# Four more stages as seven quarter products of 256 columns, and the mix loads on GpSimd's queue

## The chip, the cores and the metric

The kernel runs on one core of a Trainium2 chip. The metric is the device time of one execution in microseconds (us). A run's time is compared with the median of the runs of the kernel before, and one execution of each kernel is recorded by the hardware profiler: which instruction ran on which engine, when, and what ended the idle time ahead of it. The engines are TensorE (PE, with its weight loads PEld), VectorE (DVE), ScalarE (ACT), GpSimd (POOL) and SyncE (SP); the last two mostly issue transfers here.

## The reference

One transformer block on 512 tokens of width 1024 in fp32. A vector c gives six modulations (adaLN). The normalised and modulated input is multiplied by w_in; the columns are split into q, k, v of 16 stick-breaking heads (width 64), q, k of 4 retention heads (width 256), v and gate of those heads (width 512) and two branch gates.

```python
mod = jnp.einsum('bd,de->be', c_act, w_ada[l]) + b_ada[l]
hmix = modulate(rmsnorm(x, g_norm1[l]), shift1, scale1)
proj = jnp.einsum('bsd,de->bse', hmix, w_in[l])
sb_q, sb_k, sb_v, r_q, r_k, r_v, r_g, br = jnp.split(proj, IN_SPLITS, axis=-1)
...
# per retention head: scores with a decay mask, outputs, rms norm, times silu(gate)
# per stick-breaking head: log_sigmoid of the scores, a running sum, exp, times v
```

Both attentions are projected (w_proj_sb, w_proj_ret), weighted by the sigmoids of the branch gates, added, projected by w_out and added to x; then comes a gated feed-forward network (FFN) with its own modulation, and a final normalisation.

## The kernel before, in words

Every matrix is kept as a pair of rounded values, a high half and a low half (high = the value rounded to the fast fp32r format, low = the rest). A product is three matmuls: high x high, high x low, low x high (`mm3`, all recorded at line L229). A weight piece of 128 x 1024 elements (512 KB) is loaded by SP's queue into a buffer `raw` (three buffers) or `araw` (two), ScalarE makes its high half `whi` and VectorE subtracts to get the low half `wlo` (four buffers each; `split`, L207 and L209). The activations of the input stage are eight pairs `hs` with the features on the partitions.

Some products are already done by Strassen and Winograd's scheme: seven products of quarter size with sums of weights and of activations in place of eight. The sums of the activations, with their high and low halves, lie ready in `sacts` under the names A11, A12, A22, S1 to S4. `seven("r2", ...)` makes the values of heads 1 and 2 that way, `seven("sv", ...)` the stick-breaking values, both with 512 columns per matmul, and the FFN with 256. `low_dma` (L869, L870) is a second way to a low half: ScalarE writes the negated high half and an accumulating transfer from GpSimd's queue adds the raw weight to it.

The stages around the change, with their times in the profiled execution: the gate of head 1 (194 to 218 us), q and k of head 2, the projection of head 1 (about 240 to 262), outputs of head 2, the gate of head 2 (273 to 297), q and k of head 3, values of head 3 (319 to 341, `ret_v`), the projection of head 2, outputs of head 3, the gate of head 3 (376 to 399), the projection of head 3 (399 to 421), the stick-breaking values (`seven("sv")`, 421 to 459), then `sb_qk(0)`, a mix, `sb_qk(1)`, a mix (459 to 492), the stick-breaking heads with the remaining mixes, the loop over w_proj_sb (730 to 775), the loop over w_out and the FFN (830 to 1125). A mix reads a sum of projections back from memory (`spill`), multiplies it by a branch gate and writes it again.

`ret_gate` makes four products of 128 columns of the gate with 24 matmuls of 512 tokens each; between the second and the fourth stand a column sum and a broadcast (`ret_scale`, `bcast`) that normalise the retention output. Each silu'd gate multiplies an output tile on VectorE, which is then split into high and low halves (`s`) for the projection. Partial results of the projections are added in memory by transfers on GpSimd's queue (L816).

The adaLN modulations that are not needed at once (16 calculations) are spread over later stages by `ada_after`: two loads of 512 KB into `araw` and two dot products on VectorE (L257, 128 x 1024) each, with small additions (L260). The loop over w_proj_sb loads two tiles `r` and `t` per step, L1123 and L1124.

The program is written in a framework whose scheduler fixes the order of each engine's instructions when the program is built; at run time each engine takes them in that order and waits at the first that is not ready.

## Time and profile before

| what | value |
|---|---|
| median of 3 runs | 1174.38 us (1173.70 to 1174.75) |
| profiled execution, its own time | 1174.77 us |
| its span (first to last instruction) | 1173.1 us |
| mean granted TensorE clock | 0.998 of full speed |
| matmuls recorded | 6476 |
| ScalarE busy | 52% |

The page lists busy time by engine, the chain of work that ended last, groups of equal instructions and the transfers. A row of a group reads: line, engine, operation, output<-input, partitions x elements, xcount, then busy time in all, mean of one in ns, and the engine's idle time just ahead with what ended it. A row of the timeline reads: start, length, engine, line, operation, with the idle time ahead in brackets. A matmul's row in the timeline includes its way through the array, so its price in a row of equal ones is taken from the distance of starts. A stretch lists busy time of PE, PEld, DVE, ACT and POOL in a window.

### The profile page before, as it was taken

To read this page: it belongs to the slowest core of one execution; us is meant where nothing else is said; L and a number is where in the kernel's file an instruction comes from. 1 tells how busy PE (TensorE), PEld (TensorE's weight loads), DVE (VectorE), ACT (ScalarE), POOL (GpSimd) and SP (SyncE) were. 2 spreads that over 40 slices of the span, in tenths; PEclk is the share of its full clock that TensorE was granted. 3 is DMA by queue.
4 is the path that set the end of the run, shared out by engine and by line. 5 is a ranking of instruction groups with operands and counts; after the bars stand their busy time and mean duration, and the time that the engine had idled before them with its cause. 6 is when DMAs were issued, how large, how long until landed. Compare 5 with 4: busy or idle time off the path is not lost.

```text
span 1173.1 us, 16899 instructions
## 1 busy us (share of the span) xinstructions
PE 1156.8 (99%) x6476; PEld 1010.9 (86%) x6476; DVE 873.2 (74%) x1342; ACT 611.9 (52%) x928; POOL 50.1 (4%) x84
## 2 busy tenths in 40 slices
PE   8999999999999999999999999999999999999996
PEld 7898888888878888888888888879999999999996
DVE  7979966775764867478888688775998776777556
ACT  5444543343333444478778688354954444454433
POOL 0000000020002010000000000000100000000000
PEclk9999999999999999999999999999999999999999
DMA  9723536493566565846565545873545663565232
GB/s 358 256 68 113 185 103 208 154 260 115 161 201 176 181 159 185 232 123 180 153 173 133 153 126 179 283 235 103 113 136 179 184 161 116 148 186 152 86 89 72
DMA packets 64017, 192.88 MB, mean 164 GB/s; under 512 B 7744, under 2 KB 9920, under 8 KB 63936
## 3 DMA queue, kind: packets, MB, share of 16 engines
q1 hardware_dynamic: 56624, 172.92, 46.3%
q0 software_dynamic: 6768, 18.35, 8.8%
q8 instruction: 51, 0.84, 0.3%
q10 hardware_dynamic: 544, 0.52, 0.1%
q14 instruction: 30, 0.25, 0.1%
HBM read 146.15 MB, written 18.87 MB: 141 GB/s over the span
## 4 chain that ended last, share of the span: by engine, by line
PE 89%; DVE 4%; DMA 3%; ACT 2%; issue 1%; SPq 0%; DVEq 0%; ACTq 0%
PE ps L229 65%; PE z L229 21%; PE av L229 3%; DMA raw<-wp 2%; DMA araw<-wada 1%; DVE sraw L387 1%; ACT whi L207 1%; DVE wlo L209 1%; DMA o<-xT 0%; ACT s L207 0%; DVE wlo L418 0%; DVE t L425 0%; DVE araw L257 0%; DMA gspill<-g 0%; DVE t L476 0%
## 5 line engine op out<-in xcount | busy, mean ns | idle before, releaser
L229 PE MATMUL ps<-h,whi 128*128 128x512 f32 (+1 forms) x1410 | 416.9, 377 | 1.6 <-DVE h L209 0.8
L229 PEld LDWEIGHTS ps<-h,whi 128*128 128x128 f32 x1410 | 256.2, 188 | 47.7 <-ACT h L431 1.8
L229 PE MATMUL ps<-h,wlo 128*128 128x512 f32 (+1 forms) x705 | 262.1, 376 | 0.0
L207 ACT ACTIVATE whi<-raw 128x1024 fp32r<-128x1024 f32 (+1 forms) x122 | 127.4, 1044 | 192.3 <-PE ps L229 144.8
L209 DVE TENSOR_TENSOR wlo<-raw,whi 128x1024 fp32r<-128x1024 f32 (+1 forms) x122 | 146.6, 1204 | 61.9 <-ACT whi L207 60.8
L229 PEld LDWEIGHTS ps<-h,wlo 128*128 128x128 f32 x705 | 132.8, 188 | 23.2
L229 PE MATMUL ps<-s,whi 128*128 128x512 f32 x480 | 148.5, 390 | 0.7 <-DVE v L209 0.6
L229 PE MATMUL z<-q,whi 128*128 128x256 f32 x504 | 106.8, 283 | 0.0
L229 PEld LDWEIGHTS ps<-s,whi 128*128 128x128 f32 x480 | 89.2, 188 | 19.3 <-DVE v L209 1.0
L229 PE MATMUL ps<-s,wlo 128*128 128x512 f32 x240 | 93.4, 389 | 0.0
L207 ACT ACTIVATE s<-t 128x512 fp32r<-128x512 f32 (+1 forms) x134 | 74.4, 586 | 34.8 <-DVE t L789 21.4
L209 DVE TENSOR_TENSOR s<-t,s 128x512 fp32r<-128x512 f32 (+1 forms) x134 | 81.3, 637 | 9.6 <-ACT s L207 9.3
L229 PEld LDWEIGHTS z<-q,whi 128*128 128x128 f32 x504 | 84.9, 192 | 1.5
L1166 DVE SCALAR_TENSOR_TENSOR o<-ps,mod,o 128x512 f32<-128x512 f32 (+1 forms) x63 | 42.4, 680 | 32.6 <-PE ps L229 32.6
L229 PEld LDWEIGHTS ps<-s,wlo 128*128 128x128 f32 x240 | 45.1, 188 | 9.5
L877 ACT ACTIVATE whi<-s 128x1024 fp32r<-128x1024 f32 x33 | 34.9, 1056 | 33.6 <-PE ps L229 19.0
L229 PE MATMUL ps<-whi,h 128*128 128x512 f32 (+1 forms) x192 | 52.4, 354 | 0.0
L881 DVE TENSOR_TENSOR wlo<-s,whi 128x1024 fp32r<-128x1024 f32 x32 | 39.1, 1222 | 16.3 <-ACT whi L877 15.9
L229 PE MATMUL ps<-q,whi 128*128 128x256 f32 (+1 forms) x224 | 49.3, 313 | 0.0
L229 PE MATMUL z<-qp,whi 128*128 128x256 f32 x168 | 47.2, 283 | 0.0
L229 PE MATMUL z<-q,wlo 128*128 128x256 f32 x168 | 46.4, 283 | 0.0
L257 DVE SCALAR_TENSOR_TENSOR araw<-araw,cact 128x1024 f32<-128x1024 f32 x32 | 38.4, 1221 | 10.0 <-DMA araw<-wada 9.8
(311 smaller groups left out, 2063.1 us busy)
## 6 DMA issues: line engine op xcount, KB each, us to landing
raw<-wp SPq DMA_DIRECT2D x151, 512.0 KB, 4.0
araw<-wada SPq DMA_DIRECT2D x32, 512.0 KB, 4.5
araw<-wp SPq DMA_DIRECT2D x26, 512.0 KB, 4.6
sraw<-wada SPq DMA_DIRECT2D x16, 512.0 KB, 7.8
q<-qp SPq DMA_DIRECT2D x32, 256.0 KB, 3.7
s<-wp SPq DMA_DIRECT2D x12, 512.0 KB, 5.2
spill<-o POOLq DMA_DIRECT2D x24, 256.0 KB, 7.2
o<-xT SPq DMA_DIRECT2D x16, 256.0 KB, 3.7
```

The lines of the kernel that those rows point to most:

```text
L207: nc.scalar.activation(dst_hi, src, AF.Copy, scale=scale)
L209: return (eng or nc.vector).tensor_sub(dst_lo, src, f(dst_hi))
L229: return nc.tensor.matmul(o, lhs, rhs, start=start, stop=stop, skip_group_check=True).ins
L257: nc.vector.scalar_tensor_tensor(raw, raw, 1.0, cact, op0=ALU.mult, op1=ALU.mult, accum_out=col)
L387: nc.vector.scalar_tensor_tensor(raw, raw, 1.0, cact, op0=ALU.mult, op1=ALU.mult, accum_out=col)
L877: nc.scalar.activation(hi, t, AF.Copy)
L881: nc.vector.tensor_sub(lo, t, f(hi))
L1166: return nc.vector.scalar_tensor_tensor(x1[d][:, hv], o[:, hv], mod[:, gcol + d : gcol + d + 1], x1[d][:, hv], op0=ALU.mult, op1=ALU.add,)
```

## The change

Four stages are now made by a new function `unit`: the gates of heads 1 and 2 (`rg1`, `rg2`), the values of head 3 (`rv3`) and q and k of the stick-breaking pairs 0 and 1 together (`sb0`). A unit has 512 rows of the weight, twice, by 512 columns, twice: four raw pieces b11, b12, b21, b22 of 512 KB (512 x 256 elements each), from which seven weight operands are made (w1 to w7), and seven products of 24 matmuls with 256 columns each. Three of the operands are raw pieces, four are sums on VectorE. w3's low half is made by the negated copy and the accumulating transfer. The seven results are summed into the four quarter outputs by VectorE (with two copies by ScalarE), and each is handed to `store` as it is done. For the values the activations are the stationary operand (`tokens=True`), otherwise the weights.

`unit_gate` normalises the output tiles between the products, multiplies each by silu of its quarter outputs and splits a tile when both its halves are there. `unit_sb` splits q and k of both pairs into four tiles and spreads them over the heads by transfers when the unit is done; both mixes follow it, where one stood after each pair before. The loads and the first three operands of `sb0` are written into `seven("sv")`, ahead of its last product.

The adaLN calculations are taken from the gates of heads 1 and 2 and added to the gate of head 3 (after each of its four tiles, not after every second) and, since the same list is worked off, to the loop over w_proj_sb: the gates have 2, 2, 2 before and 0, 0, 4 now, the loop 2 before and 4 now, the projections of heads 1 and 2 four each as before. The loads of `r` and `t` in that loop go from SP's queue to GpSimd's.

```diff
--- before.py
+++ after.py
@@ -41,6 +41,15 @@
 FF_CHUNKS = ((0, 1), (1, 2), (3, 2), (5, 2), (7, 2), (9, 2))
 
 
+
+UNITS = {
+    "rg1": (C_RG + 1 * RV, C_RG + 1 * RV + 256),
+    "rg2": (C_RG + 2 * RV, C_RG + 2 * RV + 256),
+    "rv3": (C_RV + 3 * RV, C_RV + 3 * RV + 256),
+    "sb0": (C_Q, C_K),
+}
+
+
 def weight_plan():
 
     plan = []
@@ -58,6 +67,10 @@
             for c in range(2):
                 for piece in range(2):
                     add((name, half, c, piece), "w_in", half * 512 + piece * 256, 2, rng(col + c * 512, 512))
+    for name, cols in UNITS.items():
+        for half in range(2):
+            for c in range(2):
+                add(("u", name, half, c), "w_in", half * 512, 4, rng(cols[c], 256))
     for p in range(8):
         add(("sq", p), "w_in", 0, 8, rng(C_Q + p * P, P))
         add(("sk", p), "w_in", 0, 8, rng(C_K + p * P, P))
@@ -560,6 +573,9 @@
         qhl, khl = pair("qp"), pair("qp")
         split(qhl[:, 0, :], qhl[:, 1, :], qp, 0.125)
         split(khl[:, 0, :], khl[:, 1, :], kp)
+        sb_qk_spread(p, qhl, khl)
+
+    def sb_qk_spread(p, qhl, khl):
         kt_ = pair("q")
         for hf in range(2):
             r = slice(hf * HD, hf * HD + HD)
@@ -791,7 +807,7 @@
             ins = split(hl[:, 0, :], hl[:, 1, :], t)
             ys.append(hl)
             between()
-            if e % 2 and h:
+            if h == 3 or h == 1 and e % 2:
                 ada_after(ins)
         return ys
 
@@ -978,6 +994,122 @@
                 split(t4[:, :, 0:4:3, :], t4[:, :, 1:3, :], src)
             if hc:
                 nc.sync.dma_start(vspill[2 * g + n], f(vt))
+
+    def unit_raw(name, half, c, tag):
+        r = wpool.tile([P, WCOLS], F32, tag=tag, bufs=BUFS[tag], name=nm(tag))
+        nc.sync.dma_start(r, wp[WIDX["u", name, half, c]])
+        return r
+
+    def unit_ahead(name):
+
+        b11, b12, b22 = unit_raw(name, 0, 0, "raw"), unit_raw(name, 0, 1, "araw"), unit_raw(name, 1, 1, "raw")
+        w1 = sv_parts(b11)
+        nc.vector.tensor_sub(b11, b12, b11)
+        w5 = sv_parts(b11)
+        b21 = unit_raw(name, 1, 0, "araw")
+        return b11, b12, b22, b21, w1, w5, sv_parts(b21)
+
+    def unit(name, store, hooks={}, tokens=False, ahead=None):
+
+
+
+        def product(key, w, o=None):
+            ah, al = sacts[key]
+            first = o is None
+            o = ps() if first else o
+            hi, lo = (t.rearrange("p (k c) -> p k c", k=4) for t in w)
+            for i in range(2):
+                oi = o[:, i * 256 : i * 256 + 256]
+                c = slice(i * P, i * P + P)
+                for k in range(4):
+                    a, z = first and i == 0 and k == 0, i == 1 and k == 3
+                    if tokens:
+                        mm(oi, ah[k][:, c], hi[:, k, :], a, False)
+                        mm(oi, ah[k][:, c], lo[:, k, :], False, False)
+                        mm(oi, al[k][:, c], hi[:, k, :], False, z)
+                    else:
+                        mm3(oi, hi[:, k, c], lo[:, k, c], ah[k], al[k], a, z)
+            return o
+
+        hook = lambda n: hooks.get(n, lambda: None)()
+        b11, b12, b22, b21, w1, w5, w2 = ahead or unit_ahead(name)
+        x = product("A11", w1)
+        p1, p5, c22 = otile(), otile(), otile()
+        nc.scalar.activation(p1, x, AF.Copy)
+        nc.vector.tensor_sub(b11, b22, b11)
+        w6 = sv_parts(b11)
+        nc.scalar.activation(p5, product("S1", w5), AF.Copy)
+        hook(5)
+        nc.vector.tensor_sub(b12, b22, b12)
+        w7 = sv_parts(b12)
+        nc.vector.tensor_sub(b21, b21, b11)
+        x = product("A12", w2, x)
+        if 6 not in hooks:
+            store(0, 0, x)
+        w3 = sv_parts(b22, True)
+        nc.vector.tensor_add(p1, p1, product("S2", w6))
+        if 6 in hooks:
+            hook(6)
+            store(0, 0, x)
+        nc.vector.tensor_add(p5, p5, p1)
+        w4 = sv_parts(b21)
+        o = product("S3", w7)
+        nc.vector.tensor_add(c22, p5, o)
+        nc.vector.tensor_add(p1, p1, o)
+        store(1, 1, c22)
+        nc.vector.tensor_add(p1, p1, product("A22", w4))
+        store(1, 0, p1)
+        nc.vector.tensor_add(p5, p5, product("S4", w3))
+        store(0, 1, p5)
+
+    def unit_v(h):
+        vt = [pair("v") for _ in range(4)]
+
+        def store(th, c, t):
+            for b in range(2):
+                hl = vt[2 * th + b]
+                cc = slice(c * 256, c * 256 + 256)
+                split(hl[:, 0, cc], hl[:, 1, cc], t[:, b * 256 : b * 256 + 256])
+
+        unit(f"rv{h}", store, tokens=True)
+        return vt
+
+    def unit_gate(h, os_, sq):
+        y, ys, left = [], {}, {0: 2, 1: 2}
+
+        def scale():
+            r = bcast(y[0], psa())
+            for t in os_:
+                nc.vector.tensor_mul(t, t, r)
+
+        def store(th, c, t):
+            sg = tmp()
+            nc.scalar.activation(sg, t, AF.Silu)
+            for i in range(2):
+                o = os_[2 * c + i][:, th * 256 : th * 256 + 256]
+                nc.vector.tensor_mul(o, o, sg[:, i * 256 : i * 256 + 256])
+            left[c] -= 1
+            if left[c] == 0:
+                for e in (2 * c, 2 * c + 1):
+                    ys[e] = pair("s")
+                    last_low[0] = split(ys[e][:, 0, :], ys[e][:, 1, :], os_[e])
+
+        unit(f"rg{h}", store, {5: lambda: y.append(ret_scale(h, sq)), 6: scale})
+        return [ys[e] for e in range(4)]
+
+    def unit_sb(ahead=None):
+
+        hls = [[pair("s"), pair("s")] for _ in PI]
+
+        def store(th, c, t):
+            tt = slice(th * 256, th * 256 + 256)
+            for p in PI:
+                hl = hls[p][c]
+                split(hl[:, 0, tt], hl[:, 1, tt], t[:, p * 256 : p * 256 + 256], 0.125 if c == 0 else 1.0)
+
+        unit("sb0", store, ahead=ahead)
+        for p in PI:
+            sb_qk_spread(p, *hls[p])
 
     rvts = {}
 
@@ -1056,7 +1188,10 @@
         if h == 0:
             steps = sv_acts()
             sacts = next(steps)
-        ys = ret_gate(h, os_, sq, (lambda: next(steps)) if h == 0 else lambda: None)
+        if f"rg{h}" in UNITS:
+            ys = unit_gate(h, os_, sq)
+        else:
+            ys = ret_gate(h, os_, sq, (lambda: next(steps)) if h == 0 else lambda: None)
         if h < 3:
             qk = ret_qk(h + 1)
             scores = lambda: st.update(ret_scores(h + 1, qk))
@@ -1070,10 +1205,11 @@
                 nc.sync.dma_start(f(vt[b]), vspill[4 + b])
             ret_proj(1, ys, lambda i: scores() if i == 3 else None)
         elif h == 2:
-            vt = ret_v(3)
+            vt = unit_v(3) if "rv3" in UNITS else ret_v(3)
             ret_proj(2, ys, lambda i: scores() if i == 3 else None)
     act_table = ln_exp_tables()
-    seven("sv", 3, ys, sv_store)
+    sb0 = []
+    seven("sv", 3, ys, sv_store, lambda: sb0.append(unit_ahead("sb0")) if "sb0" in UNITS else None)
 
     maskc = table(consts[:, NCON + 2 * S :])
 
@@ -1091,8 +1227,11 @@
             fn, d = mixes.pop(0)
             fn(d)
 
+    if "sb0" in UNITS:
+        unit_sb(sb0[0])
     for p in PI:
-        sb_qk(p)
+        if "sb0" not in UNITS:
+            sb_qk(p)
         with tc.issue_after(act_table.ins):
             mix(1)
     for g, n in enumerate((2, 2, 4, 6)):
@@ -1120,8 +1259,8 @@
         o = ps()
         gemm(o, weight(("ps", d)), acts)
         r, t = tmp(), tmp()
-        nc.sync.dma_start(r, spill[d])
-        nc.sync.dma_start(t, gspill[d])
+        nc.gpsimd.dma_start(r, spill[d])
+        nc.gpsimd.dma_start(t, gspill[d])
         nc.vector.tensor_mul(t, t, o)
         nc.vector.tensor_add(t, t, r)
         hl = pair("h")
```

The built order of three places. First ScalarE in the gate of head 1: `whi` are high halves of weights, `t<-ps` at L777 (L1087 after) is silu, `s` the high half of a gated tile. Before:

```order
L207 ACTIVATE whi_380_1991<-raw_379_1989 128x1024
L777 ACTIVATE t_350_1860<-ps_346_1829 128x512
L207 ACTIVATE whi_391_2040<-raw_390_2038 128x1024
L777 ACTIVATE t_360_1915<-ps_356_1884 128x512
L207 ACTIVATE s_366_1932<-t_335_1771 128x512
L207 ACTIVATE s_367_1937<-t_338_1788 128x512
L207 ACTIVATE whi_394_2070<-raw_393_2068 128x1024
```

After, from the same place; L1038 and L1041 copy the first two products out of PSUM, L885 is the negated copy for w3's low half (`wlo_371`):

```order
L893 ACTIVATE whi_360_1880<-raw_346_1829 128x1024
L1038 ACTIVATE o_357_1875<-ps_356_1850 128x512
L893 ACTIVATE whi_368_1933<-araw_347_1831 128x1024
L1041 ACTIVATE o_358_1876<-ps_362_1884 128x512
L893 ACTIVATE whi_370_1962<-raw_348_1833 128x1024
L1087 ACTIVATE t_378_2010<-ps_356_1850 128x512
L885 ACTIVATE wlo_371_1963<-whi_370_1962 128x1024
L893 ACTIVATE whi_379_2015<-araw_353_1844 128x1024
```

The negated copy stands behind the silu of the first quarter output, though its own input, the high half `whi_370`, is written one place ahead of that. On TensorE the scheduler has put three quarters of S4's matmuls, which use that low half, ahead of A22's here, right behind S3's.

Second VectorE in the gate of head 3 (not a unit): `s` at L209 (L222) are the low halves of the gated tiles, `araw` at L257 (L270) the adaLN dots, `wlo` low halves of weights. Before:

```order
L209 TENSOR_TENSOR s_662_3436<-t_631_3275,s_662_3436 128x512
L209 TENSOR_TENSOR s_663_3441<-t_634_3292,s_663_3441 128x512
L257 SCALAR_TENSOR_TENSOR araw_664_3444,sm_665_3446<-araw_664_3444,cact_71 128x1024
L257 SCALAR_TENSOR_TENSOR araw_666_3449,sm_667_3451<-araw_666_3449,cact_71 128x1024
L260 TENSOR_TENSOR mod_95<-sm_665_3446,sm_70 128x1
L789 TENSOR_TENSOR t_637_3310<-t_637_3310,t_672_3485 128x512
L260 TENSOR_TENSOR mod_95<-sm_667_3451,sm_70 128x1
L788 TENSOR_TENSOR t_640_3328<-t_640_3328,av_657_3421 128x512
L209 TENSOR_TENSOR wlo_701_3598<-raw_699_3595,whi_700_3597 128x1024
L209 TENSOR_TENSOR s_673_3489<-t_637_3310,s_673_3489 128x512
```

After, from the first `s` on, with the rows between cut at the second pair of dots:

```order
L222 TENSOR_TENSOR wlo_726_3900<-raw_724_3897,whi_725_3899 128x1024
L270 SCALAR_TENSOR_TENSOR araw_682_3730,sm_683_3732<-araw_682_3730,cact_71 128x1024
L270 SCALAR_TENSOR_TENSOR araw_684_3735,sm_685_3737<-araw_684_3735,cact_71 128x1024
L273 TENSOR_TENSOR mod_95<-sm_683_3732,sm_70 128x1
L222 TENSOR_TENSOR s_692_3777<-t_650_3584,s_692_3777 128x512
L273 TENSOR_TENSOR mod_95<-sm_685_3737,sm_70 128x1
L805 TENSOR_TENSOR t_653_3602<-t_653_3602,t_702_3823 128x512
L280 SCALAR_TENSOR_TENSOR sm_686_3740<-mod_95,sm_70 128x1
L222 TENSOR_TENSOR wlo_735_3942<-raw_733_3939,whi_734_3941 128x1024
L222 TENSOR_TENSOR s_703_3827<-t_653_3602,s_703_3827 128x512
```

A second pair of dots (`araw_682`, `araw_684`) now stands ahead of the low halves of the third tile (`s_692`) and the fourth (`s_703`); before, one pair stood ahead of the third and the other behind the fourth.

Third the loads near the end of the loop over w_proj_sb. SP's queue before, where `raw<-wp` are weights and L1123 and L1124 the mix loads:

```order
L1123 DMA t_1309_6908<-spill_563 128x512
L202 DMA araw_1287_6787<-wada 128x1024
L202 DMA araw_1289_6792<-wada 128x1024
L1124 DMA t_1310_6909<-gspill_564 128x512
L202 DMA raw_1313_6918<-wp 128x1024
L1123 DMA t_1316_6948<-spill_563 128x512
L202 DMA raw_1320_6958<-wp 128x1024
```

SP's queue after, with the weights and the adaLN loads alone:

```order
L215 DMA raw_1364_7390<-wp 128x1024
L215 DMA araw_1323_7199<-wada 128x1024
L215 DMA araw_1325_7204<-wada 128x1024
L215 DMA raw_1371_7430<-wp 128x1024
L215 DMA araw_1334_7249<-wada 128x1024
L215 DMA araw_1336_7254<-wada 128x1024
L215 DMA raw_1390_7494<-wp 128x1024
```

A mix load ahead of a weight has gone from SP's queue, and two adaLN loads stand in its place; the mix loads are the only rows of GpSimd's queue between the low half for `sb0` and the first of the FFN.

## The prediction

> **What bounds the kernel now.** I read the page's head first (span, busy time by engine, shares of the chain that ended last).
>
> ```profile
> span 1173.1 us, 16899 instructions
> PE 1156.8 (99%) x6476; PEld 1010.9 (86%) x6476; DVE 873.2 (74%) x1342; ACT 611.9 (52%) x928; POOL 50.1 (4%) x84
> PE 89%; DVE 4%; DMA 3%; ACT 2%; issue 1%; SPq 0%; DVEq 0%; ACTq 0%
> ```
>
> TensorE is busy 99% of the span and carries 89% of the chain. The table of what TensorE waited for, all program, says how much waiting there is to add to or to win:
>
> ```profile
> PE z L229 <- DVE mod L450: 3.8, 1, 3.8
> PE ps L229 <- DVE h L209: 0.8, 1, 0.8
> ...
> PE ps L229 <- ACT h L431: 0.2, 1, 0.2
> ```
>
> It has 7 rows; after the first, at the start of the program, none is over 0.8 us. So TensorE's time is the program's time nearly everywhere, and a matmul saved is time saved unless a wait takes its place. The stages in question come next, as stretches: length, then busy time of PE, PEld, DVE, ACT and POOL (instructions), the granted clock, the DMA share, GB/s. In order: gate of head 1, gate of head 2, values of head 3, gate of head 3, the q and k products of the first two stick-breaking pairs with their two mixes, the loop over w_proj_sb, and the FFN.
>
> ```profile
> 194.32:218.10 23.78, 23.78 (x113) 19.84 (x112) 16.95 (x39) 7.17 (x11) 0.00 (x0) 1.00 0.57 187
> 273.40:297.20 23.80, 23.80 (x114) 19.83 (x113) 16.69 (x40) 7.16 (x11) 0.00 (x0) 1.00 0.27 86
> 318.90:340.70 21.80, 21.80 (x97) 17.76 (x95) 14.15 (x21) 7.12 (x9) 0.00 (x0) 1.00 0.45 142
> 376.00:399.30 23.30, 23.30 (x111) 19.45 (x110) 15.69 (x38) 7.48 (x11) 0.00 (x0) 1.00 0.31 91
> 458.85:491.50 32.65, 32.65 (x145) 27.04 (x144) 13.90 (x19) 11.38 (x17) 0.00 (x0) 1.00 0.89 245
> 728.00:777.00 49.00, 47.81 (x211) 39.04 (x209) 34.51 (x50) 17.59 (x22) 0.00 (x0) 1.00 0.81 271
> 830.00:1125.00 295.00, 295.00 (x2095) 278.67 (x2094) 221.29 (x250) 147.12 (x175) 16.33 (x19) 1.00 0.54 149
> ```
>
> The first five have no idle TensorE, so each is a stretch where saved matmuls count in full; VectorE is the next fullest (16.95 of 23.78 us in gate 1). The FFN is the precedent: it is already made of seven quarter products with 256 columns, and TensorE never waits in 295 us while VectorE is 75% busy.
>
> **The products.** The price of a matmul comes from runs of equal ones in the chain of waits (start, length, what):
>
> ```profile
> 53.85 7.49 PE ps L229 x62
> 207.44 48.99 PE ps L229 x216
> 850.58 5.76 PE z L229 x48
> ```
>
> 48.99 / 216 = 226.8 ns for 512 columns; 5.76 / 48 = 120.0 ns for 256 columns with the weight as the stationary side; 7.49 / 62 = 120.8 ns for 256 columns with activations stationary, as the values of head 3 have it. The old product is 96 matmuls, 96 x 0.2268 = 21.77 us. A unit is 7 x 24 = 168, so 168 x 0.1200 = 20.16 us (gain 1.61) or 168 x 0.1208 = 20.29 us (gain 1.48, values). Four units: 3 x 1.61 + 1.48 = 6.31 us less TensorE work. It lies on the path.
>
> A rule speaks against that. The Trainium skill, "TensorE: Matmul & The Clock Gate", section "Back-to-back issue gap", gives 81 ns per matmul at 128 columns and 131 ns at 512 for a sustained stream of weight load and matmul, so cost grows far less than in proportion to columns; an estimate on the line between them is 98 ns at 256, by which 168 matmuls of 256 would cost 16.5 us against 12.6 us for 96 of 512, and the change would lose. This trace does not agree: 226.8 and 120.0 ns, a ratio of 0.53, which is near the isolated gap of the same section.
>
> **What the units add off TensorE.** The rows are groups of instructions (xcount | busy, mean ns | idle before):
>
> ```profile
> L209 DVE TENSOR_TENSOR wlo<-raw,whi 128x1024 fp32r<-128x1024 f32 x118 | 143.9, 1222 | 61.6 <-ACT whi L207 60.5
> L207 ACT ACTIVATE whi<-raw 128x1024 fp32r<-128x1024 f32 x118 | 124.9, 1058 | 188.8 <-PE ps L229 143.3 <-issue 21.2 <-DMA raw<-wp 13.8
> L257 DVE SCALAR_TENSOR_TENSOR araw<-araw,cact 128x1024 f32<-128x1024 f32 x32 | 38.4, 1221 | 10.0 <-DMA araw<-wada 9.8
> L788 DVE TENSOR_TENSOR t<-t,av 128x512 f32<-128x512 f32 x16 | 10.6, 680 | 0.0
> ```
>
> VectorE: 4 low halves become 6 low halves and 4 weight sums, 6 more of 1.22 us = 7.3; 6 adds of 128x512 at 0.68 = 4.1; together 11.4 us per unit. ScalarE: 4 high halves become 7 and a negated copy, 4 more of 1.06 = 4.2, and two copies out of PSUM of about half that: 5.3 us per unit. The weights' bytes stay as they are (4 x 512 KB). ScalarE was busy 7 to 11 us in each of those stretches and takes this beside the matmuls. VectorE is tighter. Gates 1 and 2 lose two adaLN calculations each (2 dots of 1.22 us apiece, 4.9 us a gate), so gate 1 comes to 16.95 + 11.4 - 4.9 = 23.5 us of summed durations in 23.78 - 1.61 = 22.2 us. Neighbours on VectorE overlap by some 7% (two weight halves in a row take 2.35 us in a row below, so the second costs 1.13), so it is just full; what is left over runs on into the q/k product behind it, whose weights are split early. I cost the arithmetic itself at nothing, hidden beside the matmuls, in gates 1 and 2 and in the values of head 3 (there 14.15 + 11.4 against 20.3 us; the surplus of 5 us must be done in the q/k stage ahead, where the first weights of the unit can be prepared; if not, it costs up to those 5 us, which belongs to the rivals), and price below the places where one late result meets a matmul.
>
> **Low half of b22 by transfer, gates 1 and 2.** S4 uses a low half made by a negated copy on ScalarE and an accumulating transfer from GpSimd's queue. In a gate S4 is begun after five products and the two small ones of the normalisation, 5 x 2.88 + (23.78 - 21.77) = 16.4 us in, its low half a third of a us later. The negated copy stands behind the silu of A12's result. A12 ends at 3 x 2.88 + some 0.7 = 9.4; silu of 128x512 half of 1.06, then the copy: 11.0. The transfers of that kind, L870, wherever they run (from issue to landing):
>
> ```profile
> DMA to landing us min/median/max: 4.5/5.2/8.5
> ```
>
> It lands at 15.5, 16.2 or 19.5 against 16.7: a stall of 0 at the median and 2.8 at the maximum. I take 0.5 in each of the two gates, nearer the median; ends 0 and 5.6 for both. It can't be below 0, as TensorE waits for nothing there now; that holds for every term but the last. In the values of head 3 and the pairs no silu stands ahead of the copy and S4 comes last: nothing.
>
> **The adaLN dots, moved.** There are now none in gates 1 and 2, four in gate 3 instead of two, four in the loop over w_proj_sb instead of two. Each needs two loads of 512 KB into a pair of buffers (araw) that the units use too, and each dot that waits for its load holds VectorE with all that stands behind it:
>
> ```profile
> 256.74 1.23 DVE L257 SCALAR_TENSOR_TENSOR araw<-araw,cact 128x1024 f32<-128x1024 f32 x1 [5.46 <-DMA araw<-wada]
> 352.55 1.23 DVE L257 SCALAR_TENSOR_TENSOR araw<-araw,cact 128x1024 f32<-128x1024 f32 x1 [3.16 <-DMA araw<-wada]
> 261.80 2.35 DVE L210 SCALAR_TENSOR_TENSOR s<-z,con,s 128x256 fp32r<-128x256 f32 x4
> 265.58 1.63 PE L229 MATMUL z<-s,v 128*128 128x256 f32 x10
> araw<-wada SPq DMA_DIRECT2D x32, 512.0 KB, 4.5
> ```
>
> Before gate 2 a weight sum of the unit now stands between the last dots of the projection of head 1 and the low halves of the scores, which end at 261.80 + 2.35 = 264.15 now. TensorE comes to them at 265.58, with unit 1 at 263.97. If the loads come no sooner, that is 0.2 late, with the sum ahead 1.3; if they move along, nothing: 0 to 1.3, I take 0.3, since a load that lands sooner frees all of it. Gate 3 is the place I trust least:
>
> ```profile
> 392.07 1.28 DVE L209 TENSOR_TENSOR s<-t,s 128x512 fp32r<-128x512 f32 x2
> 393.28 1.22 DVE L257 SCALAR_TENSOR_TENSOR araw<-araw,cact 128x1024 f32<-128x1024 f32 x1
> ...
> 396.91 1.22 DVE L209 TENSOR_TENSOR wlo<-raw,whi 128x1024 fp32r<-128x1024 f32 x1
> 398.04 0.69 DVE L209 TENSOR_TENSOR s<-t,s 128x512 fp32r<-128x512 f32 x1
> ...
> 402.51 0.69 DVE L209 TENSOR_TENSOR s<-t,s 128x512 fp32r<-128x512 f32 x1 [0.70 <-ACT s L207]
> 394.53 1.47 SPq L202 DMA_DIRECT2D araw<-wada  x2
> ```
>
> The second pair of dots will stand ahead of the low halves of the third and fourth gated tile, and its buffers come free only with the first pair of dots. Its loads, issued as in the last row, land 4.5 us later or more: 399 to 402. Then 2.3 us of dots, a 1.1 us weight half and the fourth tile's half follow, so that one is ready at 402.9 to 406.8 instead of at 403.2. The projection of head 3 needs it at about 403.5. Stall 0 to 3; I take 1.2, below the middle, since 4.5 is the median of such loads.
>
> **Stick-breaking pairs.** Both pairs' unit now runs ahead of both mixes, and its preparation inside the last products of the seven-product stage in front. Around the seam VectorE has:
>
> ```profile
> 456.66 2.35 DVE L209 TENSOR_TENSOR wlo<-raw,whi 128x1024 fp32r<-128x1024 f32 x2
> 458.93 1.28 DVE L1048 TENSOR_TENSOR t<-t,ps 128x512 f32<-128x512 f32 x2
> ...
> 461.59 1.43 DVE L209 TENSOR_TENSOR s<-t,s 128x256 fp32r<-128x256 f32 x4
> 474.05 0.60 SPq L568 DMA_DIRECT2D q<-qp  x1
> ```
>
> The unit's third prepared weight (for S2) stands behind the old stage's stores and three sums. By those durations its low half is ready near 468.4; TensorE comes to it at 468.0. I take 0.5 (0 to 1.5). The spread of q and k over the heads is 16 transfers from SP's queue behind the unit, 0.6 us an issue (last row of the fence). In the old times the unit runs from 458.85 to 479.0, its last store is split 1.5 later, and the first head's four transfers are issued by 482.9 and, at the 4.5 us of the adaLN loads, which are larger, landed by 487.4. The two mixes (2 x 24 x 0.2268 = 10.9 us) cover that until 489.9: nothing. Were one mix alone ahead, it would cost 3 us.
>
> **The w_proj_sb loop.** The mix loads go from SP's queue to GpSimd's, which issues nothing near. Here TensorE had the two waits in the next rows, 1.2 us, at the end of the loop; a weight load in the chain takes 7.47 us where the median is 4.0, and the DMA share is 0.81.
>
> ```profile
> 775.62 0.51 PE L229 MATMUL ps<-h,whi 128*128 128x512 f32 x1 [0.35 <-ACT h L207]
> 776.96 0.50 PE L229 MATMUL ps<-h,whi 128*128 128x512 f32 x1 [0.84 <-DVE h L209]
> 743.99 7.47 DMA raw<-wp
> raw<-wp SPq DMA_DIRECT2D x151, 512.0 KB, 4.0
> ```
>
> For the better: SP's queue stalls no longer on a buffer for a mix load with a weight behind it, which could end both waits (-1.2). For the worse: two more adaLN calculations bring 4 x 512 KB, at 271 / 0.81 = 335 GB/s some 6 us of all DMA engines out of 9 that were free, and 4.9 us of dots beside 34.5 of 49; price up to +2. I take +0.3, near the middle. The Trainium skill, "DMA: Bandwidth & Descriptors", section "Issuing engines are not separate DMA queues", holds that all issuers share the same 16 DMA engines and that a second issuer saves only sequencer time, small beside the transfer; by it the gain's end falls away, the part is 0 to 2, so 1.0 at the middle, and the sum 0.7 us higher. No run here shows it yet.
>
> **Sum.** -6.31 + 0.5 + 0.5 + 0.3 + 1.2 + 0.5 + 0.3 = -3.0 us. The profiled execution took 1174.77 us (span and 1.67 us around it), so 1171.8; it lies 0.4 over the median of the runs, 1174.38, so the forecast is 1171.4 us.
>
> **Rivals.** Full gain: every prepared value is in time, as in the FFN (295 us without a wait), and the loop's two waits go: -6.31 - 1.2 to -6.31 + 1.5, that is 1166.9 to 1169.6. For it speaks the FFN; against it that VectorE is 75% busy there and full in the gates.
>
> The waits eat the gain: each taken at the upper part of its bounds, 1.5 per gate, 1, 2, 1 and 0.8, which sum to 7.8; the case is 4 to 8.6 us of waits, 1172.1 to 1176.7. For it speaks the long rows of waits on adaLN loads; against it that VectorE's waits so far cost TensorE nothing.
>
> Slower: VectorE held by a load. Where units and adaLN share the two araw buffers (entry of gate 2, gate 3 into the projection, the seam at 459, the w_proj_sb loop) a dot or sum waits for a load issued only when the buffer came free, 3.16 to 5.46 us as shown, and VectorE, full in these stages, has no slack left to make it good. At three of the four places 4.3 us each makes +12.9: 1174.4 - 6.3 + 12.9 = 1181.0. It is slower from 8.7 us on (6.31 + 2.35), 2.9 at each of three places. Against it: most loads are issued stages ahead.
>
> Slower matmuls: 256 columns at a price that does not halve. From (21.77 + 2.35 / 4) / 168 = 133 ns a matmul on, without any wait, the kernel is slower; at 140 ns a unit is 23.5 us, 4 x 1.75 = +7.0, and with the 3.3 us of waits 1184.7. The two rows of 120.0 and 120.8 ns speak against it. By the page on TensorE above a unit would cost 16.5 / 12.6 of the old product, 28.5 us, which is +27 us and 1201.
>
> **Chances.** Forecast (1.5 to 4 us of waits, 1169.6 to 1172.1) 0.42; full gain 0.14; waits eat the gain 0.22; VectorE held by loads 0.19; slower matmuls 0.03. A measurement tells 0.2%, 2.35 us, from no change, so faster is below 1172.0 and slower above 1176.7: faster 0.42 + 0.14 = 0.56, same 0.22, slower 0.22. The range, 1167.0 to 1178.0, holds the first three cases and a little of the fourth (0.04); above it 0.18 is left out, held loads and slow matmuls. The forecast's own range is 1169.6 to 1172.1.
>
> **What would show it.** Right: runs of 24 matmuls of 120 ns in the four stages; the gates' stretches at about 22.5 us, the head-3 values at 20.3; the w3 row on GpSimd landing about 5 us after its issue with a wait of under 1 us at S4. Wrong: in the table of TensorE's waits a row of several us on a weight half, on a gated low half near 401, or on an araw load; GpSimd's landing over 7 us in a gate; matmul runs of 256 columns over 125 ns. The prediction falls if the new waits sum to more than 4 us or less than 1.5.

## The result

The changed kernel takes 1180.56 us in the median of 8 runs (1175.74 to 1183.53), the kernel before 1174.34 (8 runs, 1172.99 to 1174.77): the ratio is 1.0054, 95% interval 1.0038 to 1.0070. It is slower by some 6 us, clear of the 0.2% bound, where a gain of 3 us was forecast, and it lies above the top of the range, 1178.0.

The runs also differ from one another, which those of the kernel before hardly do. The profiled execution is the shortest of the eight, 1175.74 us, at a mean granted TensorE clock of 0.997; the other seven stand at 0.992 to 0.996. So its profile shows only a part of the loss, the waits; the lowered clock is in the profile of the first experiment. The head of its page:

```profile
span 1174.0 us, 17613 instructions
PE 1152.0 (98%) x6764; PEld 1020.1 (87%) x6764; DVE 916.0 (78%) x1406; ACT 632.3 (54%) x960; POOL 66.8 (6%) x104
PE 81%; DVE 8%; DMA 7%; issue 2%; ACT 2%; POOL 0%; DVEq 0%; SPq 0%; ACTq 0%; POOLq 0%
```

TensorE is busy 4.8 us less, but its share of the chain has gone from 89% to 81%; VectorE and the transfers have taken it. The matmuls did what was forecast. The stretches of the gate of head 1, the gate of head 2, the values of head 3, and then the loop over w_proj_sb (length, busy PE, PEld, DVE, ACT, POOL, granted clock, DMA share, GB/s):

```profile
193.47:216.43 22.96, 22.26 (x186) 22.01 (x184) 16.97 (x39) 10.15 (x13) 1.00 (x1) 1.00 0.69 214
275.21:297.55 22.34, 22.25 (x186) 22.01 (x184) 16.07 (x37) 9.55 (x12) 0.86 (x1) 1.00 0.44 122
319.33:339.49 20.16, 20.16 (x170) 20.15 (x168) 17.76 (x28) 12.38 (x18) 0.85 (x1) 1.00 0.50 139
727.00:777.00 50.00, 46.75 (x207) 38.29 (x206) 38.93 (x62) 17.66 (x23) 5.89 (x11) 1.00 0.89 303
```

Busy TensorE is 22.26 and 22.25 us in the gates instead of 23.8, and 20.16 for the values instead of 21.8: 1.5 us less in each gate and 1.6 for the values. VectorE was full in none of these. The units themselves cost nothing but 0.7 us in the first gate, 0.09 in the second and 0.26 in the stick-breaking pairs (at 468 us). What is lost is lost elsewhere. TensorE's waits (in total, times, longest):

```profile
PE z L242 <- DVE mod L463: 3.8, 1, 3.8
PE ps L242 <- ACT s L220: 3.3, 1, 3.3
PE z L242 <- POOL s L601: 2.4, 3, 1.0
PE ps L242 <- DVE wlo L897: 0.8, 2, 0.5
PE ps L242 <- DMA wlo<-raw: 0.7, 1, 0.7
PE ps L242 <- ACT o L828: 0.7, 1, 0.7
```

The first row is the start-up that was there before. The others are new. Beside the 0.26 us of the pairs they sit at four places: the outputs of head 2 (264 to 268 us, 2.6 us in all with a wait of 0.2), the start of the stick-breaking values (425 to 427, 1.2), the first gate (0.7) and the start of the w_proj_sb loop (732 to 735, 3.3). From 50 to 1150 us TensorE is idle 8.55 us, against 1.99 before (the stretch less its busy time): +6.6 us, a little more than the matmuls give, -6.3.

The two profiled executions differ by +0.97 us, although TensorE was 0.97 us ahead at the start (the first long run of matmuls at 52.88 instead of 53.85 us). So some 1.7 us more were lost than the idle time shows. Of these, 1.0 us is hidden in the waits at the outputs of head 2, since idle time is counted only from where the matmul ahead has gone through the array: from the start of the last matmul ahead of these outputs to the start of the first behind them it is 11.58 us (263.63 to 275.21), before 7.94 (265.36 to 273.30). That is 3.64 us more for 2.60 us of idle time. The remaining 0.7 us were not followed up.

How the three larger waits come about is in the chain of waits of the same profile (start, length, what), first at the outputs of head 2, then ahead of the stick-breaking values:

```profile
245.23 1.16 DVE araw L270 x2
246.40 5.62 DMA araw<-wada
253.31 6.47 DMA araw<-wp
259.80 1.24 DVE raw L1007
262.20 1.22 DVE wlo L897
265.69 2.13 POOL s L601 x4
...
404.88 7.61 DMA araw<-wada
412.51 1.23 DVE araw L270 x2
413.78 9.13 DMA araw<-wp
424.14 1.23 DVE wlo L897
...
727.03 6.83 DMA t<-t
```

The unit of the next gate loads its piece b12 into an `araw` buffer, which comes free only when the last adaLN dot but one of the projection is done (252.05 us, itself 3.2 us late for its load). That load takes 6.5 us, and VectorE stands still for 3.8 of them. The weight sum that uses it (L1007), a second sum (L1043) and a weight's low half stand on VectorE ahead of the first low halves of head 2's scores, a third sum (L1039) between these and the rest. So a sum whose product begins at 278 us holds back scores needed at 264.

The POOL rows at L601 (L585 in the kernel before) are GpSimd's causal masks on these scores, eight per head, the last step ahead of TensorE's products. All eight at the outputs of head 2, before and after:

```profile
262.41 2.41 POOL L585 TENSOR_SCALAR_AFFINE_SELECT s<-s 128x256 fp32r<-128x256 f32 x8 [3.48 <-DVE s L210]
263.89 4.41 POOL L601 TENSOR_SCALAR_AFFINE_SELECT s<-s 128x256 fp32r<-128x256 f32 x8 [7.38 <-DVE s L223]
```

They begin 1.5 us later than before and end 3.5 us later. Two of the eight last 1.49 and 1.39 us, where none took over 0.40 before. These two run beside VectorE's third sum (264.26 us, 1.21) and a weight's low half (266.44, 1.21), and TensorE's two longest waits there, 0.98 and 0.96 us, end right behind them. So VectorE's operations did harm twice: they came ahead of the low halves, and they ran beside the masks.

At 404 us it is the same pair of buffers: four adaLN calculations in the gate of head 3 instead of two push the second of two loads of the stick-breaking values' raw weights to 413.8, where it takes 9.1 us. At 727 us the last head's small transfer `t<-t`, whose kind took 2.2 us in the median, takes 6.8, since five mix loads of 256 KB have gone ahead of it on GpSimd's queue.

### The profile page after: what moved, and what is told of

Read it like the earlier page. It is cut to its first block, busy times and chain, and to the rows that moved or that the text cites. A ratio compares the mean times of both kernels' runs of the same rounds, so it can differ in the third digit from the quotient of the medians.

```text
span 1174.0 us, 17613 instructions
## 1 busy us (share of the span) xinstructions
PE 1152.0 (98%) x6764; PEld 1020.1 (87%) x6764; DVE 916.0 (78%) x1406; ACT 632.3 (54%) x960; POOL 66.8 (6%) x104
## 4 chain that ended last, share of the span: by engine, by line
PE 81%; DVE 8%; DMA 7%; issue 2%; ACT 2%; POOL 0%; DVEq 0%; SPq 0%; ACTq 0%; POOLq 0%
PE ps L242 58%; PE z L242 21%; DMA araw<-wada 3%; PE av L242 2%; DVE araw L270 2%; DMA araw<-wp 1%; DMA t<-t 1%; DMA wlo<-raw 1%; DVE wlo L897 1%; DVE wlo L222 1%; DVE sraw L400 0%; ACT s L220 0%; DVE s L222 0%; POOL s L601 0%; DVE t L438 0%
## 5 line engine op out<-in xcount | busy, mean ns | idle before, releaser
L242 PE MATMUL ps<-h,whi 128*128 128x512 f32 (+1 forms) x1362 | 383.7, 365 | 0.3
L242 PEld LDWEIGHTS ps<-h,whi 128*128 128x128 f32 x1362 | 242.8, 189 | 38.7 <-ACT h L444 1.7
L242 PE MATMUL ps<-h,wlo 128*128 128x512 f32 (+1 forms) x681 | 245.1, 364 | 0.0
L220 ACT ACTIVATE whi<-raw 128x1024 fp32r<-128x1024 f32 (+1 forms) x106 | 110.0, 1040 | 127.7 <-PE ps L242 88.9
L242 PEld LDWEIGHTS ps<-h,wlo 128*128 128x128 f32 x681 | 128.5, 189 | 19.4
L222 DVE TENSOR_TENSOR wlo<-raw,whi 128x1024 fp32r<-128x1024 f32 (+1 forms) x106 | 126.7, 1199 | 17.0 <-ACT whi L220 16.1
L222 DVE TENSOR_TENSOR s<-t,s 128x512 fp32r<-128x512 f32 (+1 forms) x134 | 81.1, 637 | 8.6 <-ACT s L220 8.1
L893 ACT ACTIVATE whi<-raw 128x1024 fp32r<-128x1024 f32 x36 | 38.1, 1057 | 54.5 <-PE ps L242 41.0
L242 PE MATMUL ps<-q,whi 128*128 128x256 f32 (+1 forms) x320 | 66.8, 304 | 0.0
L242 PEld LDWEIGHTS ps<-q,whi 128*128 128x128 f32 x320 | 51.9, 191 | 2.5
L270 DVE SCALAR_TENSOR_TENSOR araw<-araw,cact 128x1024 f32<-128x1024 f32 x32 | 38.9, 1222 | 15.1 <-DMA araw<-wada 14.9
L242 PE MATMUL ps<-q,wlo 128*128 128x256 f32 (+1 forms) x160 | 48.8, 305 | 0.3 <-DVE wlo L897 0.3
```

The costliest lines, as they stand in the source:

```text
L220: nc.scalar.activation(dst_hi, src, AF.Copy, scale=scale)
L222: return (eng or nc.vector).tensor_sub(dst_lo, src, f(dst_hi))
L242: return nc.tensor.matmul(o, lhs, rhs, start=start, stop=stop, skip_group_check=True).ins
L270: nc.vector.scalar_tensor_tensor(raw, raw, 1.0, cact, op0=ALU.mult, op1=ALU.mult, accum_out=col)
L893: nc.scalar.activation(hi, t, AF.Copy)
```

## The experiments

### The changed kernel once more

No edit.

> The changed kernel once more, to see where its executions differ: the profiled one took 1175.74 us at a mean granted clock of 0.997, seven others 1179.7 to 1183.5 at 0.992 to 0.996. Theory (mix loads): the waits are the same in all, the longest at the start of the w_proj_sb loop, 3.25 us in the profile; where it grows past some 4 us TensorE's clock is lowered behind it, and the run is 4 to 8 us longer. So 1175 to 1183 us again, and if this profile is of a long run, a stretch of lower clock behind the start of that loop. Rival (adaLN loads): the long wait and the lower clock lie at the projection of head 3 or its start of the stick-breaking values, 400 to 427 us.

Measured: 1181.82 us (1180.62 to 1185.04, 4 runs), ratio 1.0073 (1.0057 to 1.0088). This time the profile is of the longest execution, 1185.04 us, at a mean clock of 0.991. Its stretches of 2 us at the outputs of head 2, in the same columns as above:

```profile
264.00:266.00 2.00, 1.23 (x7) 0.72 (x5) 2.00 (x4) 1.69 (x4) 0.62 (x2) 1.00 0.00 0
266.00:268.00 2.00, 0.79 (x3) 0.38 (x3) 2.00 (x4) 1.73 (x3) 2.00 (x5) 1.00 0.01 4
268.00:270.00 2.00, 1.04 (x4) 0.84 (x5) 1.14 (x2) 0.00 (x0) 2.00 (x4) 0.69 0.00 0
270.00:272.00 2.00, 2.00 (x7) 1.81 (x7) 0.00 (x0) 0.00 (x0) 1.45 (x2) 0.50 0.56 56
272.00:274.00 2.00, 2.00 (x9) 1.90 (x9) 1.58 (x2) 0.63 (x1) 0.00 (x0) 0.50 1.04 133
274.00:276.00 2.00, 2.00 (x8) 1.77 (x8) 0.40 (x2) 0.00 (x0) 0.00 (x0) 0.61 0.45 81
276.00:278.00 2.00, 2.00 (x15) 1.86 (x14) 1.30 (x3) 0.63 (x1) 0.00 (x0) 1.00 0.00 0
```

TensorE waits 2.9 us among a few matmuls, and behind that it is busy but granted half its clock for 6.8 us: 2 x (0.31 + 0.50 + 0.50 + 0.39) = 3.4 us lost. The same follows the waits at 428 to 432 us (2.4 us, then 1.7 lost) and at 740 to 743 us (2.8 us, then 1.7 lost). In all this execution has 10.5 us of idle TensorE and 6.8 us of lost clock: 8.5 + 6.8 - 6.3 = +9.0 us over the kernel before, where the spans differ by 10.2. So the waits are at the same places in a long and in a short run, as the theory had it; two are of much the same length, the one at 428 us has grown from 1.2 to 2.4, and one of 1.0 at 699 us is new. The lowered clock stands behind all three, not behind the loop's start alone. It makes 6.8 of the 9.3 us between the two executions of this kernel.

### The loop's loads back on SP's queue

```diff
-        nc.gpsimd.dma_start(r, spill[d])
-        nc.gpsimd.dma_start(t, gspill[d])
+        nc.sync.dma_start(r, spill[d])
+        nc.sync.dma_start(t, gspill[d])
```

> The changed kernel with the loads of the w_proj_sb loop back on SP's queue. Theory (mix loads): the last head's transfer is again 2 to 3 us instead of 6.8, the wait of 3.25 us at the loop's start goes, and with it the long runs: 1171 to 1174 us in all runs, within 1 us of each other. Rival (adaLN loads, or the units themselves): still 1176 to 1183 us with the same spread.

Measured: 1181.50 us (1177.13 to 1183.25, 4 runs), ratio 1.0060 (1.0038 to 1.0082). The theory that the mix loads are the one cause falls. The wait at the loop's start has gone, but two more adaLN calculations now stand in the same queue as the mix loads, and a w_out weight is late:

```profile
PE z L242 <- POOL s L601: 2.7, 4, 1.0
PE ps L242 <- DVE wlo L897: 2.1, 2, 1.9
PE ps L242 <- ACT whi L220: 1.9, 1, 1.9
```

The first two rows are the waits at 264 and 428 us; the third is the new one, 2.4 us idle at 776 to 780 with another of 0.5, and 1.7 us of clock lost behind it. One wait has taken the place of the other.

### The loop's loads on GpSimd's queue, alone

The kernel before with the 16 loads of the loop on GpSimd's queue (the edit above, the other way round).

> The kernel before with these 16 loads alone put on GpSimd's queue. Theory (mix loads): a wait of 2 to 4 us at the loop's start, 1176 to 1181 us with a spread of several us. Rival (the units or adaLN): 1173 to 1175 us, as before, no spread.

Measured: 1176.77 us (1175.09 to 1178.82, 10 runs), ratio 1.0024 (1.0014 to 1.0033). Part of the theory holds. The move alone makes a wait of 3.5 us at the loop's start, ends the 1.19 us of waits at its end, and spreads the runs, in a kernel in which no matmul is changed. In the profile 1.7 us of lost clock follow the wait. So a stretch of lowered clock can follow a wait in a kernel without units.

### The loop's loads on SP's queue and the adaLN calculations at their old places

```diff
-            if h == 3 or h == 1 and e % 2:
+            if e % 2 and h:
...
                     last_low[0] = split(ys[e][:, 0, :], ys[e][:, 1, :], os_[e])
+                ada_after(last_low[0])
```

(and the loop's loads as in the second experiment)

> The changed kernel with the loads back on SP's queue and the adaLN calculations back at their old places (two each in the gates of heads 1, 2 and 3, two in the w_proj_sb loop). Theory: against the one before, 1 to 2 us less in the projection of head 3 and the stick-breaking values (1.2 us of waits at 425 us), against up to 2 us more in the gates of heads 1 and 2, where VectorE gets 4.9 us of dots back: 1170 to 1174 us. Rival (adaLN loads decide): 1168 to 1170 us, 4 us or more under the variant with the new places.

Measured: 1185.16 us (1182.63 to 1185.55, 4 runs), ratio 1.0092 (1.0077 to 1.0107). Both expectations fail. The wait at 425 us has gone, but the longer line of adaLN loads in front shifts those of the next projection: the scores of head 3 now stand behind dots that wait for their loads, TensorE is idle 5.1 us at 370 to 377 us, and 3.4 us of clock are lost behind that. The waits at the outputs of head 2 stay, 3.6 us with 3.4 of clock.

### Two units alone

The kernel before with the values of head 3 and the stick-breaking pairs as units:

```diff
 UNITS = {
-    "rg1": (C_RG + 1 * RV, C_RG + 1 * RV + 256),
-    "rg2": (C_RG + 2 * RV, C_RG + 2 * RV + 256),
     "rv3": (C_RV + 3 * RV, C_RV + 3 * RV + 256),
     "sb0": (C_Q, C_K),
 }
```

> The kernel before with only the values of head 3 and the first two stick-breaking pairs as units; gates, adaLN places and the queue of the loop's loads as before. Theory (each unit saves its 1.5 to 1.6 us of matmuls, and what is lost is lost at three waits of the other parts, each followed by a stretch of half clock): 3.1 us of matmuls less, waits of up to 0.6 us more, no lowered clock: 1171 to 1172.5 us, runs within 1 us of each other. Rival (units themselves hold up TensorE): 1175 us or more.

Measured: 1173.07 us (1170.56 to 1176.19, 10 runs), against 1173.88 before; ratio 0.9995 (0.9986 to 1.0005). Between the two: 3.1 us of matmuls are saved and most of it is lost again at one place that was not expected, the scores of head 3 at 364 to 368 us. The adaLN loads that follow the unit of the values come later, the last two from 351.97 us on instead of 345.77, and VectorE's low halves of the scores stand behind their dots. That the unit holds the `araw` buffers longer is the likely reason, not a shown one. In the profile, which is of the longest run, that is 1.8 us idle and 1.7 us of clock.

### Head 2's scores ahead of the unit's first sum

```diff
+        if name == "rg2":
+            with tc.issue_after(score_low[0].ins):
+                nc.vector.tensor_sub(b11, b12, b11)
+        else:
             nc.vector.tensor_sub(b11, b12, b11)
```

(`score_low` is the last low half of the scores; the loop's loads are on SP's queue)

> The changed kernel with the loop's loads on SP's queue (as in the second run) and one edge more: the unit of the gate of head 2 makes its first weight sum behind the low halves of head 2's scores on VectorE. Theory: the waits at 264 to 269 us (2.7 us in the second run) and the half clock behind them (some 3 us) go, those at 430 us (2.8 us) and 776 us (1.9 us) stay with theirs: 1175 to 1178 us. Rival (the wait there comes from the scores' chain itself, or the time comes back as a wait on the unit's second weight): 1179 to 1183 us.

Measured: 1174.67 us (1170.45 to 1176.45, 10 runs), ratio 0.9998 (0.9986 to 1.0009), 6.8 us less than the second experiment for one edge between two instructions. The idle time at 264 us has gone, and so has the half clock behind it: 2.7 and 3.4 us, together 6.1. The weight sums now begin only when the last mask runs, and no mask takes over 0.40 us. The two other places are left as expected: 2.4 us idle and 1.7 of clock at 420 to 428 us, 2.6 and 1.7 at 768 to 776.

### The adaLN calculations placed anew

As the last one, with two in each of the gates of heads 2 and 3, two among the stick-breaking heads, two in the loop:

```diff
-            if h == 3 or h == 1 and e % 2:
+            if e % 2 and h:
...
+                if h == 2:
+                    ada_after(last_low[0])
...
             mix(n - n // 2)
+            if g < 2:
+                ada_after(last_low[0])
```

> As the run above, with the adaLN calculations placed anew: none in the gate of head 1, two in the gates of head 2 and of head 3, two among the stick-breaking heads, two in the w_proj_sb loop (four each in the projections, as in all). Theory: the waits at 430 us (adaLN loads in the projection of head 3 hold back the stick-breaking values' raw weights) and at 776 us go as well, no lowered clock, and the four units keep their 6.3 us less some 1.5 us of small waits: 1168.5 to 1171 us. Rival (VectorE is too full for four units whatever the order): 1174 us or more, with new waits in the gates.

Measured: 1178.75 us (1178.24 to 1179.87, 5 runs), ratio 1.0043 (1.0031 to 1.0056). The places at 425 and 776 us are good, the latter with 0.8 us left and no lowered clock. But head 3's scores are late again, as in the fourth experiment. The chain there:

```profile
355.36 7.02 DMA araw<-wada
362.40 1.25 DVE araw L270 x2
363.83 1.23 DVE araw L270 x2
365.36 1.23 DVE wlo L222
367.12 1.74 POOL s L601 x7
```

5.7 us idle and 3.4 of clock. A calculation among the heads whose dot waited 2.6 us for its load cost another 1.0.

### Scores of head 3 first, loads among the heads early

```diff
-            if h in (1, 2):
+            if h == 1 or h == 2 and i < 2:
                 ada_after(low)
+            elif h == 2 and i == 3:
+                ada_after(score_low[0])
...
-            nc.scalar.activation(sg, t, AF.Silu)
+            with tc.issue_after(negated[0].ins):
+                nc.scalar.activation(sg, t, AF.Silu)
...
+                if held:
+                    ada_after(done, held.pop())
...
             mix(n - n // 2)
+            held.append(ada_loads(later[0]))
```

(the loads are issued at the end of a group of heads, the dots, `ada_after`, behind the next group's first head, `done`; one calculation less is left to the projection of head 2, and it stands behind head 3's scores)

> All four units, the loop's loads on SP's queue, head 2's scores ahead of the unit's first sum on VectorE, and the adaLN calculations kept away from full places: projection of head 1 four, gates of heads 2 and 3 two each, projection of head 2 three, the last of them behind head 3's score low halves, three among the stick-breaking heads with loads a head ahead of the dots, w_proj_sb loop two. ScalarE's negated copy stands ahead of the silu in the gates. Theory: of the waits of the run before, 5.7 us at 362 to 376 us and 1.0 at 620 us go, and with them the 3.4 us of half clock; small ones of 0.3 to 0.8 us stay, none followed by half clock: 1168.5 to 1170.5 us, runs within 1.5 us. Rival (VectorE too full: the time comes back at a new place): 1173 us or more, with a wait of over 1.8 us somewhere between 200 and 500 us.

Measured: 1172.84 us (1170.92 to 1174.86, 11 runs), ratio 0.9990 (0.9981 to 0.9999). The wait for the scores, those among the heads, and with the silu behind the negated copy the 0.7 us in the first gate are gone. One of 2.7 us is left, and the edit itself has made it:

```profile
PE z L242 <- DVE mod L276: 2.7, 1, 2.7
361.35 4.19 POOL L604 TENSOR_SCALAR_AFFINE_SELECT s<-s 128x256 fp32r<-128x256 f32 x8 [0.17 <-DVE s L223]
```

The calculation moved behind the scores has its dots on VectorE from 362.7 to 365.2 us, beside GpSimd's masks (L604 here), and one of these lasts 1.29 us. The first row puts the wait down to VectorE, but the same profile has TensorE's weight loads wait 2.9 us for the masks. VectorE's copies of head 3's outputs, which stand behind the dots, begin only at 367.4 us, after TensorE has gone on at 365.4, so they are not what it waited for.

### Two loads of the loop on SP's queue, the rest on GpSimd's

As the last one, with one calculation among the heads (placed as in the seventh), four in the loop, and:

```diff
+        queue = nc.sync if d < 2 else nc.gpsimd
+        queue.dma_start(r, spill[d])
+        queue.dma_start(t, gspill[d])
```

> As the run above, but with one adaLN calculation among the heads and four in the w_proj_sb loop, and there the loads of the first two steps on SP's queue behind the last head's transfer, of the other six on GpSimd's. Theory: with only one mix load ahead of the last head's transfer that transfer takes under 4 us and the wait at the loop's start stays under 1 us; SP's queue has two more adaLN loads ahead of the first w_out weight, so a wait of 0 to 2.4 us near 773 us, with 1.7 us of half clock if it is over 1.8: 1168.5 to 1173.5 us. Rival (any load of the loop on GpSimd's queue costs the wait at its start): a wait of 2 to 3.5 us at 730 us again, 1173 to 1176 us.

Measured: 1170.72 us (1167.38 to 1173.67, 7 runs), ratio 0.9971 (0.9958 to 0.9985). The last head's transfer takes 4.9 us at the most, TensorE waits nowhere at the loop's start, and 0.2 us at its end. The loads on GpSimd's queue do no harm where only one goes ahead of that transfer. The 2.7 us at 363 us are still there, with two masks of 1.29 and 1.27 us, each beside one of the two dots.

### The dots behind the copies

```diff
             sq = sumsq(ot, sq)
...
+        if h == 3:
+            ada_after(copied)
         return os_, sq
```

(`copied` is the last copy of the outputs; the call behind head 3's scores is taken out)

> The run on the loop's queue with one adaLN calculation moved again: the third of the projection of head 2 has its dots on VectorE behind the last copy of head 3's outputs instead of ahead of the first. Theory: the one wait left over 0.3 us, 2.67 us at 363 to 366 us, goes, and with it the half clock that followed it in some runs: 1167 to 1169 us, runs within 2 us of each other. Rival (the time comes back in the gate of head 3, whose normalisation stands behind the dots): a wait of 1 to 3 us near 380 us, 1169.5 to 1171.5 us.

Measured: 1168.15 us (1165.83 to 1169.47, 5 runs), against 1173.77 before; ratio 0.9950 (0.9937 to 0.9962). This kernel is faster than both. The head of its page and, in the second block, all of TensorE's waits:

```profile
span 1164.1 us, 17607 instructions
PE 1149.7 (99%) x6764; PEld 1020.2 (88%) x6764; DVE 915.0 (79%) x1406; ACT 632.9 (54%) x960; POOL 63.6 (5%) x100
PE 93%; DVE 4%; issue 1%; ACT 1%; DMA 1%; DVEq 0%; ACTq 0%
```

```profile
PE z L242 <- DVE mod L463: 3.8, 1, 3.8
PE z L242 <- ACT t L1731: 0.3, 1, 0.3
PE ps L242 <- DVE wlo L903: 0.3, 1, 0.3
PE ps L242 <- DVE wlo L222: 0.2, 1, 0.2
PE ps L242 <- ACT h L444: 0.2, 1, 0.2
```

With the dots away, head 3's masks are short again:

```profile
360.43 2.23 POOL L601 TENSOR_SCALAR_AFFINE_SELECT s<-s 128x256 fp32r<-128x256 f32 x8 [0.16 <-DVE s L223]
```

VectorE does the same work as in the changed kernel, 915 us, and TensorE is idle 0.7 us between 50 and 1150 us, 1.3 less than in the kernel before. So VectorE was not too full for four units. What cost the time was the order of its instructions and of the loads that they wait for.

### The same order without the units

```diff
-UNITS = {
-...
-}
+UNITS = {}
```

> The same places of the adaLN calculations, the same queues in the w_proj_sb loop and the same edges, but none of the four units: gates, values and stick-breaking q and k as in the kernel before. It measures what the units are worth by themselves. Theory (a unit saves 1.48 to 1.61 us of matmuls and nothing is hidden otherwise): 6.3 us over the run above less its small waits of 0.5 us, so 1172.5 to 1174.5 us. Rival (the gain of that run comes from the new places, not from the units): within 2 us of the run above.

Measured: 1176.56 us (1174.63 to 1178.05, 11 runs), ratio 1.0022 (1.0013 to 1.0031), 2 us above what the theory gave. The rival falls: with the units the same arrangement takes 8.4 us less, their 6.3 us of matmuls and about 2 more. The profile has 2.3 us idle from 50 to 1150 us and no lowered clock there; 1.6 of the idle time lies at the loop's end, where the tenth experiment has none. Why this arrangement is 2.8 us slower than the kernel before in the median was not settled. Of the 2.1 us between the two profiles 0.8 lies in the w_proj_sb loop and 1.1 at the end of the program.

## Why the prediction was wrong

**Products.** Right: 1.61 and 1.48 us were forecast per unit, 1.5 in each gate and 1.6 for the values were measured, and 8.4 us separate the last two experiments. By the estimate from the two figures of the Trainium skill, "TensorE: Matmul & The Clock Gate", section "Back-to-back issue gap", the change would have lost here; the trace of the changed kernel does not agree: 168 matmuls of 256 columns in 20.16 us are 120 ns each.

**VectorE's arithmetic at nothing.** Right, as far as it runs beside matmuls: no wait of over 0.1 us in the gates and the values is for a sum or a low half of VectorE's, and the tenth experiment does all of it with 0.7 us of waits in all. Beside GpSimd's masks it was not free (next but one).

**Low half of b22 by transfer.** Right: 0.7 and 0.09 us for 0.5 and 0.5. With the copy ahead of the silu no wait is left there.

**Entry of gate 2.** Wrong: 0.3 forecast with 0 to 1.3, 2.6 to 2.9 us of idle time measured, 3.6 by the starts of the matmuls. The step took one weight sum ahead of the scores at its own 1.1 us. It left out that the sum waits for a load of its own, which can only be issued when a dot has freed the buffer: VectorE stood still for 3.8 us. That is the mechanism of the slower rival, at the place it named first. It also had one sum there where two and a weight's low half came, and the masks on GpSimd, two of which took some 1.1 us more beside VectorE's work, are in no step and no rival.

**Gate 3 into the projection.** Wrong in place, and near in size by luck: 1.2 forecast, 1.2 to 2.4 measured, but 20 us later, at the stick-breaking values, whose raw weights use the same buffers as the two calculations more. The gated tiles themselves were in time. (The durations that the step names put the fourth tile at 403.1 to 406.1 us; the text has 402.9 to 406.8.)

**Pairs.** 0.5 forecast, 0.26 measured.

**The w_proj_sb loop.** Wrong: 0.3 forecast with -1.2 to +2. The two waits at its end went, -1.2, as the good end had it; but 2.8 to 3.3 us came at its start, which no step looked at; in the first profile +2.1 together, just outside the bounds. The text counted what the mix loads no longer hold up on SP's queue, and not what they pass when they wait on a queue of their own: the order behind the last head's transfer was lost.

**The price of a wait.** This is the step that failed most: every wait was put into the sum at its own length. In the long execution of the first experiment three of them were followed by 1.7 to 3.4 us of half clock each, in the short one none; the mean clocks of the other runs, 0.992 to 0.996, lie between. The forecast's waits came to 3.3 us; measured were 6.6 to 8.5 us more of idle TensorE than before, and up to 6.8 us of lost clock. By the prediction's own sign, more than 4 us of new waits, it falls in either run. The slower rival, with 0.19, had the mechanism (a dot or a sum waiting for a load in `araw`), at two of the places, and 1181.0 us as its time. That the time came so near is luck: the clock and the loop's start, not a third such place, brought it there.

## What to carry to other kernels

Where TensorE has no slack, an instruction added to another engine is priced by what it waits for, not by what it takes: look for each sum or dot at the load that it needs, at the buffer that this load needs, and at what is queued behind it. Look too at what runs beside it on GpSimd. Count a cluster of waits of some 2 us or more on TensorE at more than its length; at the places listed below the lost clock made it 1.6 times as much on the whole and 2.3 times at the worst. And a transfer moved to an idle queue goes as early as its buffer allows, so ask which transfer on the path it now goes ahead of.

## What the runs showed of the hardware

The lost clock comes in steps. Between 50 and 1150 us of the profiles of the kernels here (the changed one and the first nine experiments) there are 17 places where TensorE's waits within a few us come to 1.8 us or more; 13 of them are followed by a stretch at half clock that costs 1.70 to 1.72 us or 3.40 to 3.42 us, that is 3.4 or 6.8 us long, and 4 by none (2.6 and 3.3 us in the changed kernel's first profile, twice 2.7 in the eighth and ninth experiment). Their waits come to 51.5 us in all, the lost clock behind them to 30.7. None of the clusters of 1.5 us or less in these stretches was followed by any. The first 50 us do not fit so well: the wait of 3.6 to 3.8 us with which each execution begins was followed by no step, and in the seventh experiment a step of 1.70 us stands at 16.9 us behind waits of 0.4 and 0.1 us. The waits at the same place of the changed kernel have no step in one execution and one or two in another, and this is the larger part of the difference between the two that were profiled.

GpSimd's masks last longer beside some of VectorE's work. A mask takes 0.29 to 0.40 us in the kernel before, and as little beside VectorE's low halves of the scores (128 x 256, one input from a matmul's result). Beside sums, dots and low halves of 128 x 1024 elements single masks took 1.27 to 1.49 us in the changed kernel and the ninth experiment, about as long as the operation beside them (1.21 to 1.30 us). Why is not shown here.

The Trainium skill, "TensorE: Matmul & The Clock Gate", section "What's actually happening", has the clock halve after an idle window of some 3.4 us and says that the windows run freely. The trace agrees with the length of the step and with the chance in it, and differs in one thing: in ten of the thirteen cases no single wait reached 3.4 us. At 264 to 269 us, in the stretches shown above, waits of at most 1.0 us with single matmuls between them were enough.
